# Seven products in place of eight: gate and up of a SwiGLU feed-forward by blocks of two by two

## The chip, the cores and the metric

The kernel runs on one core of one Trainium2 chip. The metric is the time of one execution on the device in microseconds (us). The core has a matrix engine (PE), a vector engine (DVE), a scalar engine (ACT), a general engine (POOL) and queues for transfers (DMA), the one of which SyncE fills (SP's) carries the weights. Each engine works through its own instructions in order and waits on semaphores for the others. SBUF is the on-chip memory of 128 partitions; PSUM holds the results of matmuls.

## The reference, cut to what matters

Two layers of mixer and feed-forward on 512 tokens of width 1024, then a last RMSNorm. The change is in the feed-forward part (`D_FF` = 2816):

```python
def rmsnorm(x, g):
    y = x * lax.rsqrt(jnp.mean(x * x, axis=-1, keepdims=True) + NORM_EPS)
    return y * g

def swiglu(xn, w_gate, w_up, w_down):
    return (jax.nn.silu(xn @ w_gate) * (xn @ w_up)) @ w_down

def reference(x, positions, ...):
    h = x
    for layer in range(DEPTH):                       # 2
        h = h + mixer(rmsnorm(h, mixer_norm_g))      # attention, not touched
        h = h + swiglu(rmsnorm(h, ffn_norm_g[layer]), ffn_w_gate[layer], ffn_w_up[layer], ffn_w_down[layer])
    return rmsnorm(h, final_norm_g)
```

## The kernel before, in words

Everything is kept transposed: `h` holds the residual stream as 8 tiles of 128 features by 512 tokens. Products are made of three matmuls: each operand is split into a rounded high part (one copy on ACT) and a low part (one subtraction on DVE), and high·high, high·low and low·high are summed in PSUM (`mm3`). `xo` holds the two parts of `h` times the norm's gain; the norm's factor per token is not in it. It is computed while the first product runs (`rstd_cols`, `rstd_rows`) and lies in `rbc`, 128 equal rows of 512 tokens.

Gate and up are made in 22 blocks `f` of 128 columns each. A block has two slabs of weights, gate and up, of 128 x 1024 numbers (8 pieces of K by 128 columns). `slab` loads one from HBM into `wraw` (512 KB, SP's queue, 2 buffers), ACT copies it to the high half of `whl` (4 buffers) and DVE makes the low half. Then 24 matmuls of 512 columns run into a bank `ps_g` (3 buffers). For gate DVE multiplies the bank by `rbc` into `gs`, ACT applies silu in place; for up DVE multiplies by `rbc` into `us`, multiplies that by `gs`, and ACT and DVE split the product into `ht[f]`. The down projection then sums over the 22 `ht` for each of 8 blocks `n` of outputs, and `residual` adds the bank to `h`. In the last layer the last block is done in two halves of 256 tokens (`final`).

The order of every engine's instructions is not the order of this code. `Sched.run` plans all of them: it walks through time with a cost for each instruction, takes on each engine the ready one with the highest rank (the longest costed path behind it, where PE's instructions keep the order in which they are written), gives out buffers in order, and emits the result. So a cost in the plan that differs from the chip's changes no result, but the order in which an engine's instructions wait on each other. Buffers of a feed-forward part lie in a memory scope that opens only when those before it are done with (the number behind the buffers in `tag`).

Of the kernel before, what the change touches and what calls it, by code (L numbers as in the profile page):

```python
# [62 lines left out]
class Sched:  # L63
# [32 lines left out]
    def run(self, opened, emit):  # L96
# [45 lines left out]
        while n_done < len(ops):  # L142
            best = None
            for e in "TVAGS":
                te = None
# [39 lines left out]
            if o.dma:  # L185
                eng[e] = st + cost
                dma_free = max(dma_free, st + cost + 600) + o.dma / 360.0
                end = dma_free + 900
# [66 lines left out]
def trunk(ctx, tc, xT, pos, consts_in, gv, lamv, wv0, wqk0, wo0, wgu0, wd0, wv1, wqk1, wo1, wgu1, wd1, out):  # L255
# [588 lines left out]
    def ffn(L, wgu, wd, gi_next):  # L844
        rbc = None
        ht = [buf(f"ht{L}") for _ in range(NF)]
        for f in range(NF):
# [33 lines left out]
        for n in range(NC):  # L881
# [17 lines left out]
    def final(n, ws, down):  # L899

        rb = buf("rbc1")

        def part(t0, tn):
# [25 lines left out]
            for c in (0, 4, 2, 6):  # L929
                o = buf("fo")  # L930
                for z in range(2):
                    src = lambda c=c, z=z: h.t[:, c + z, cols]
# [72 lines left out]
    def open_scope(sc):  # L1005
        if sc - 1 in stacks and sc > 1:
            stacks.pop(sc - 1).close()
        es = ExitStack()
        sb = es.enter_context(tc.tile_pool(name=f"sb{sc}", bufs=1))
        pp = es.enter_context(tc.tile_pool(name=f"pp{sc}", bufs=1, space=PSUM)) if sc == 0 else None  # L1010
        for t, (s, n) in tags.items():
            if s == sc:
                for i in range(n):
                    if shapes[t][0] is None:
                        phys[t, i] = "none"
                    else:
# [81 lines left out]
```

## Time and profile before

| | |
|---|---|
| runs | 1228.51, 1230.77, 1231.13 us; median 1230.77 us |
| profiled execution | 1229.38 us, of which the span is 1227.6 us |
| busy share of the span | PE 98%, DVE 55%, ACT 49%, POOL 12% |
| gate and up of layer 0 | from 250.85 us; its second block and those after it in the loop take 10.88 us each |
| down of layer 0 | 492 to 612 us |
| gate and up, down of layer 1 | 855 to 1094 us, to 1216 us |
| granted clock of PE | 1.00 (2.4 GHz) from 4 to 1219 us |

How to read it: times in the trace are from the span's start. "Idle before, releaser" beside a group is how long its engine stood just before these instructions and whose work ended that. The duration of a matmul in a row is longer than its distance to the next one, since matmuls overlap; what a row of many matmuls gives is the length of the whole run and their count.

### The profile page before, as it was taken

Reading aid. Unit: us, or ns where it says so; the run is one execution under the profiler, and the core shown is the slowest. Engines: PE = TensorE matmul, PEld = TensorE weight load, DVE = VectorE, ACT = ScalarE, POOL = GpSimd, SP = SyncE. Lnnn points to the kernel's source line nnn. Section 1 sums busy time; section 2 is a strip of 40 time slices with the busy share of each in tenths; the row PEclk is TensorE's granted clock in tenths of the full one; section 3 lists DMA queues with packets and bytes.
Section 4 is the critical chain, followed back from the end, with each engine's and each line's share of the span. In section 5 each row is a group of like instructions: output and inputs, shape, how many; then the busy total and the mean of one; then the engine's idle time right before and its main releaser. Section 6 shows DMA issues by size and latency. Waiting matters only on the chain.

```text
span 1227.6 us, 15958 instructions
## 1 busy us (share of the span) xinstructions
PE 1204.9 (98%) x5994; PEld 1014.3 (83%) x5994; DVE 672.8 (55%) x1404; ACT 598.8 (49%) x1039; POOL 150.9 (12%) x138
## 2 busy tenths in 40 slices
PE   9999999999999999999999999999999999999997
PEld 7889788888888888888897787888888888888887
DVE  7876987544444444333246988975444444443332
ACT  7877987542332323222357888875323323232221
POOL 1222331210000000000122334423000000000000
PEclk9999999999999999999999999999999999999998
DMA  8775755523233333333578657545232233333322
GB/s 252 185 171 140 162 136 113 138 86 102 87 103 91 98 103 97 97 95 95 132 182 180 144 132 172 117 124 137 86 103 89 100 101 89 103 93 97 95 77 69
DMA packets 47260, 146.49 MB, mean 119 GB/s; under 512 B 5840, under 2 KB 9040, under 8 KB 47184
## 3 DMA queue, kind: packets, MB, share of 16 engines
q1 hardware_dynamic: 38832, 116.08, 31.1%
q0 software_dynamic: 8064, 29.36, 13.8%
q8 instruction: 47, 0.77, 0.3%
q14 instruction: 29, 0.24, 0.1%
q10 hardware_dynamic: 288, 0.04, 0.0%
HBM read 134.98 MB, written 2.10 MB: 112 GB/s over the span
## 4 chain that ended last, share of the span: by engine, by line
PE 85%; DVE 8%; DMA 3%; issue 2%; ACT 1%; POOL 1%; SPq 0%; POOLq 0%; ACTq 0%; DVEq 0%
PE ps_g L351 75%; PE ps_s L351 3%; PE ps_o L351 2%; PE ps_t L351 2%; PE ps_t L354 2%; DMA kk<-kk 1%; DVE lg L716 1%; DVE lg L332 1%; DVE a L329 1%; DMA wraw<-wqk 1%; DVE kk L329 1%; DVE sh L675 1%; DVE lg L324 1%; DVE pt L329 1%; DVE qs L329 1%
## 5 line engine op out<-in xcount | busy, mean ns | idle before, releaser
L351 PE MATMUL ps_g<-xo,whl 128*128 128x512 f32 x2832 | 669.6, 391 | 0.0
L351 PEld LDWEIGHTS ps_g<-xo,whl 128*128 128x128 f32 x2832 | 526.3, 188 | 105.3
L320 ACT ACTIVATE whl<-wraw 128x1024 fp32r<-128x1024 f32 (+1 forms) x248 | 255.3, 1044 | 494.3 <-PE ps_g L351 357.6
L351 PE MATMUL ps_g<-ht,whl 128*128 128x512 f32 (+1 forms) x1122 | 241.3, 377 | 0.0
L351 PEld LDWEIGHTS ps_g<-ht,whl 128*128 128x128 f32 x1122 | 202.0, 188 | 38.6
L329 DVE TENSOR_TENSOR whl<-wraw,whl 128x1024 fp32r<-128x1024 f32 (+1 forms) x136 | 162.0, 1191 | 97.6 <-ACT whl L320 97.6
L329 DVE TENSOR_TENSOR us<-ps_g,rbc 128x512 f32<-128x512 f32 x44 | 30.4, 692 | 142.3 <-PE ps_g L351 142.3
L351 PE MATMUL ps_g<-whl,xo 128*128 128x256 f32 x672 | 92.4, 286 | 0.0
L351 PEld LDWEIGHTS ps_g<-whl,xo 128*128 128x128 f32 x672 | 86.5, 191 | 1.4 <-DVE xo L332 0.2
L329 DVE TENSOR_TENSOR gs<-ps_g,rbc 128x512 f32<-128x512 f32 x44 | 30.4, 692 | 98.8 <-PE ps_g L351 93.0
L346 ACT ACTIVATE lg<-lg,col 128x128 f32<-128x128 f32 (+3 forms) x128 | 70.9, 555 | 10.0 <-DVE col L716 8.8
L351 PE MATMUL ps_g<-ot,whl 128*128 128x512 f32 x288 | 73.6, 396 | 0.0
L329 DVE TENSOR_TENSOR h<-ps_g,h 128x512 f32<-128x512 f32 (+1 forms) x29 | 19.1, 671 | 89.2 <-PE ps_g L351 89.2
L351 PE MATMUL ps_s<-kk,qs 128*128 128x128 f32 (+3 forms) x256 | 62.1, 324 | 3.5 <-DMA kk<-kk 2.5
L351 PEld LDWEIGHTS ps_g<-ot,whl 128*128 128x128 f32 x288 | 52.9, 188 | 10.1
L389 POOL DMA_DIRECT2D whl<-wv x14 | 12.3, 882 | 373.4 <-ACT whl L320 372.4
L716 DVE CUSTOM_DVE_ANT_0 lg<-ps_s,cc 128x128 f32<-128x128 f32 (+3 forms) x96 | 45.4, 482 | 14.5 <-PE ps_s L351 11.6
L351 PEld LDWEIGHTS ps_s<-kk,qs 128*128 128x128 f32 x256 | 42.8, 189 | 12.5 <-DVE col L716 3.4
L329 POOL TENSOR_TENSOR fo<-h,rbc 128x256 f32<-128x256 f32 x4 | 2.9, 734 | 363.5 <-ACT rbc L320 363.5
L354 PE MATMUL ps_t<-cc,lg 128*128 128x128 f32 x240 | 40.5, 277 | 7.1 <-DVE lg L332 4.5
L329 DVE TENSOR_TENSOR pt<-ps_t,pt 128x128 fp32r<-128x128 f32 (+1 forms) x96 | 45.4, 480 | 2.4 <-ACT pt L320 1.7
L329 POOL TENSOR_TENSOR sh<-sh,sk 128x512 f32<-128x512 f32 x28 | 38.7, 1383 | 60.3 <-DVE sh L675 50.9
(135 smaller groups left out, 1065.1 us busy)
## 6 DMA issues: line engine op xcount, KB each, us to landing
wraw<-wgu SPq DMA_DIRECT2D x88, 512.0 KB, 3.5
wraw<-wd SPq DMA_DIRECT2D x32, 512.0 KB, 3.5
wraw<-wqk SPq DMA_DIRECT2D x30, 512.0 KB, 6.8
whl<-wqk POOLq DMA_DIRECT2D x30, 512.0 KB, 7.3
kk<-kk SPq DMA_DIRECT2D x64, 128.0 KB, 4.7
wraw<-wo SPq DMA_DIRECT2D x16, 512.0 KB, 4.8
wraw<-wv SPq DMA_DIRECT2D x14, 512.0 KB, 6.6
whl<-wv POOLq DMA_DIRECT2D x14, 512.0 KB, 7.6
```

Source lines behind the costliest of these rows:

```text
L320: A.activation(out_(), in_(), AF.Copy, scale=sc)
L324: V.tensor_scalar(out_(), in_(), sc, None, OP.mult)
L329: lambda e: E[e].tensor_tensor(out_(), a(), b(), o), r, w)
L332: op([("V", vtt(n, 1))], lambda e: V.scalar_tensor_tensor(out_(), a(), s(), b(), o0, o1), r, w)
L346: A.activation(out_(), in_(), f, scale=scale, **kw)
L351: lambda e: T.matmul(out_(), l(), r_(), start=start, stop=stop), r, w)
L354: op([("T", 108)], lambda e: T.transpose(out_(), in_(), ident()), r + [(cc, None)], w)
L389: op([("G", 1100)], lambda e: G.dma_start(w.t[:, 1, :], src, accum_op=OP.add), [(w, (1, 0))], [(w, (1, 0))], dma=2 * 1024 * 512)
L675: op([("V", vtt(512))], lambda e: V.stream_shuffle(sh.t, p.t, swap), P, [(sh, None)])
L716: op([("V", vtt(w) + 10)], lambda e: V.tensor_tensor_reduce(lg.t[:, :w], p.t[:, :w], mask[0]()[:, 512 - w:], -0.125, 3.0e38, OP.add, OP.mi ...
```

## The change

In layers 0 and 1 alike, blocks `f` = 2 to 16 (15 of 22) compute gate and up together as the product of a matrix of two by two blocks with another: A11, A12 are the two K halves of gate's slab, A21, A22 those of up's, and X11, X12, X21, X22 are the normed input cut into two halves of K (4 tiles each) and two of tokens (256 each). In place of eight products of blocks there are seven (`p1` to `p7`), each of 12 matmuls of 256 columns, with sums of weight blocks and of input blocks as operands:

- the sums of input blocks are made once for a layer, after block 0 (`sums_of_x`): 16 scaled copies of 256 columns on ACT into `hr`, 8 additions of 512 columns ("VG": on DVE or POOL, as the planner places them; here 6 and 2), and 8 splits of 512 columns into `tf`
- the sums of weight blocks are made for each block: up's slab lands in `wu`, and a POOL DMA that accumulates adds its second half to its first (256 KB, line 931); POOL makes three further sums of 512 columns (`s23`, `s4`). What is split into high and low is `w1` (gate as loaded), `w2` (`wu`), `w3` (`s23`), all three of 1024 columns in `whl`, and `w4` (`s4`, 512 columns, in `wf`)
- the seven products lie in 256 columns of seven banks (`ps_g` three times, `ps_s` twice, `ps_t`, `ps_o`); one copy on ACT and eight additions of 256 columns on DVE make gate into `cg` and up into `cu`. Then come gate times `rbc`, silu and the product with up, as before
- of blocks 2 to 5 the product is split into `hd` at once; of blocks 6 to 16 it stays in `hr` and is split into `hh` from block 17 on, when the buffers of the scheme are done with

Up is no longer multiplied by `rbc`, in any block. Instead the result of the down projection is, per token, before it is added to `h`: one more DVE instruction of 512 columns for each `n` (of 256 for each half of the last). In plain blocks DVE has one instruction fewer. The planner gets a delay for the accumulating DMA (`late`) and scopes that overlap.

```diff
     def ffn(L, wgu, wd, gi_next):
...
+        def plain(f):
...
-                tt("V", lambda g=g: g.t, lambda p=p: p.t, lambda: rbc.t, OP.mult, 512, [(p, None), (rbc, None)],
-                   [(g, None)])
...
+                    tt("V", lambda: g.t, lambda p=p: p.t, lambda: rbc.t, OP.mult, 512, [(p, None), (rbc, None)], [(g, 0)])
+                    func(lambda: g.t, lambda: g.t, AF.Silu, 512, SET, [(g, 0)])
+            tt("V", lambda: u.t, lambda: p.t, lambda: g.t, OP.mult, 512, [(p, None), (g, 0)], [(u, 0)])
+            parts(f, lambda: u.t, [(u, 0)])
...
+        def product(p, w, o, x):
+            for c in range(4):
+                for n, (a, b) in enumerate(((0, 0), (0, 1), (1, 0))):
+                    ap, tok = x(b, c)
+                    mm(lambda: p.t[:, :256], lambda a=a, c=c: w.t[:, a, o + c * 128:o + c * 128 + 128], ap, 256,
+                       c + n == 0, c == 3 and n == 2, [(w, (a, 0)), tok], [(p, None)])
+
+        def winograd(f):
+            a1, a2, s23, s4 = buf("wraw"), buf(f"wu{L}"), buf(f"s23{L}"), buf(f"s4{L}")
...
+            dma(lambda: a2.t, lambda: A2, (), [(a2, 0), (a2, 1)], 2 ** 19)
+            op([("G", 1100)], lambda e: G.dma_start(a2.t[:, k1], A2[:, k2], accum_op=OP.add), [(a2, 0)], [(a2, 0)],
+               dma=2 ** 19, late=4500.0)
+            dma(lambda: a1.t, lambda: A1, (), [(a1, 0), (a1, 1)], 2 ** 19)
+            w1, w3, w2, w4 = buf("whl"), buf("whl"), buf("whl"), buf(f"wf{L}")
...
+            both(w1, a1, 1024, halves(a1))
+            tt("G", lambda: s23.t[:, k1], lambda: a2.t[:, k1], lambda: a1.t[:, k1], OP.subtract, 512,
+               [(a2, 0), (a1, 0)], [(s23, 0)])
+            tt("G", lambda: s23.t[:, k2], lambda: a2.t[:, k2], lambda: s23.t[:, k1], OP.subtract, 512,
+               [(a2, 1), (s23, 0)], [(s23, 1)])
+            both(w3, s23, 1024, halves(s23))
+            tt("G", lambda: s4.t, lambda: s23.t[:, k1], lambda: a1.t[:, k2], OP.subtract, 512, [(s23, 0), (a1, 1)],
+               [(s4, None)])
+            both(w2, a2, 1024, halves(a2))
+            both(w4, s4, 512, [(s4, None)])
+            p1, p6, p2, p7, p5, p4, p3 = [buf("ps_" + n) for n in "gsgtgos"]
...
+            product(p1, w1, 0, xb(0, 0))
+            copy("A", u0, q(p1), 256, P(p1), [(u, 0)], psum=True)
+            product(p6, w3, 0, xt(1))
+            add(g1, u0, p6, (g, 1), [(u, 0)], OP.add)
+            product(p2, w1, 512, xb(1, 0))
+            add(g0, u0, p2, (g, 0), [(u, 0)], OP.add)
+            product(p7, w3, 512, xt(2))
+            add(u0, g1, p7, (u, 0), [(g, 1)], OP.add)
+            product(p5, w2, 0, xt(0))
+            add(u1, u0, p5, (u, 1), [(u, 0)], OP.subtract)
+            add(g1, g1, p5, (g, 1), [], OP.subtract)
+            product(p4, w2, 512, xt(3))
+            add(u0, u0, p4, (u, 0), [], OP.add)
+            product(p3, w4, 0, xb(1, 1))
+            add(g1, g1, p3, (g, 1), [], OP.subtract)
+            tt("V", lambda: g.t, lambda: g.t, lambda: rbc.t, OP.mult, 512, [(rbc, None)], halves(g))
+            func(lambda: g.t, lambda: g.t, AF.Silu, 512, SET, [(g, 0), (g, 1)])
+            if f < ND:
+                tt("V", lambda: u.t, lambda: u.t, lambda: g.t, OP.mult, 512, halves(g), halves(u))
+                parts(f, lambda: u.t, halves(u))
+                return
...
+            if f < NP or f >= NP + NS:
+                plain(f)
+                if f == 0:
+                    sums_of_x()
+            else:
+                x = winograd(f)
...
             p = buf("ps_g")
             down(n, ws, p, 0, 512)
-            residual(p, n)
+            t = buf(f"cu{L}")
+            tt("V", lambda t=t: t.t, lambda p=p: p.t, lambda: rbc.t, OP.mult, 512, [(p, None), (rbc, None)], [(t, 0)])
+            tt("V", lambda n=n: h.t[:, n, :], lambda t=t: t.t, lambda n=n: h.t[:, n, :], OP.add, 512, [(t, 0)], [(h, n)])
```

On PE, in the middle of layer 0's gate and up, two groups of 24 matmuls (one block: gate, then up) stood before:

```order
L351 MATMUL ps_g_0_82<-xo_0_64,whl_2_74 128x512 x24
L351 MATMUL ps_g_1_83<-xo_0_64,whl_3_75 128x512 x24
```

In the changed kernel the third block, the first of the scheme, and the start of the fourth stand there as follows (seven groups of 12 for a block; `xo` are input blocks as they are, `tf` sums of them, `whl` and `wf` the split weights):

```order
L358 MATMUL ps_g_0_82<-xo_0_64,whl_2_74 128x256 x12
L358 MATMUL ps_s_0_85<-tf0_0_2505,whl_3_75 128x256 x12
L358 MATMUL ps_g_1_83<-xo_0_64,whl_2_74 128x256 x12
L358 MATMUL ps_t_0_87<-tf0_0_2505,whl_3_75 128x256 x12
L358 MATMUL ps_g_2_84<-tf0_0_2505,whl_0_72 128x256 x12
L358 MATMUL ps_o_0_89<-tf0_0_2505,whl_0_72 128x256 x12
L358 MATMUL ps_s_1_86<-xo_0_64,wf0_0_2506 128x256 x12
L358 MATMUL ps_g_0_82<-xo_0_64,whl_1_73 128x256 x12
L358 MATMUL ps_s_0_85<-tf0_0_2505,whl_2_74 128x256 x12
```

What moved: a block has 84 matmuls of 256 columns in place of 48 of 512, into seven banks in place of two; `p6`, second in the block, already needs `w3` (`whl_3` in the first block), and `p5` and `p4` need `w2`.

On DVE, a block in the middle of layer 0's gate and up had these rows before (up's eviction and its product with gate, low part of a slab, low part of `ht`, gate's eviction, low part of a slab):

```order
L329 TENSOR_TENSOR us0_0_2568<-ps_g_0_82,rbc0_0_2564 128x512
L329 TENSOR_TENSOR us0_0_2568<-us0_0_2568,gs0_0_2565 128x512
L329 TENSOR_TENSOR whl_1_73<-wraw_1_71,whl_1_73 128x1024
L329 TENSOR_TENSOR ht0_3_2545<-us0_0_2568,ht0_3_2545 128x512
L329 TENSOR_TENSOR gs0_1_2566<-ps_g_1_83,rbc0_0_2564 128x512
L329 TENSOR_TENSOR whl_2_74<-wraw_0_70,whl_2_74 128x1024
```

In the changed kernel the rows of a later block of the scheme, interleaved with the last ones of the block before (`cu0_0`, `cg0_0` and the other way round for `_1`), are:

```order
L336 TENSOR_TENSOR cu0_1_2500<-cg0_1_2498,ps_t_1_88 128x256
L336 TENSOR_TENSOR whl_0_72<-wu0_1_2509,whl_0_72 128x1024
L336 TENSOR_TENSOR cu0_1_2500<-cu0_1_2500,ps_g_2_84 128x256
L336 TENSOR_TENSOR cg0_1_2498<-cg0_1_2498,ps_g_2_84 128x256
L336 TENSOR_TENSOR cu0_1_2500<-cu0_1_2500,ps_o_0_89 128x256
L336 TENSOR_TENSOR hd0_4_2483<-cu0_0_2499,hd0_4_2483 128x512
L336 TENSOR_TENSOR whl_1_73<-wraw_1_71,whl_1_73 128x1024
L336 TENSOR_TENSOR cg0_1_2498<-cg0_1_2498,ps_s_1_86 128x256
L336 TENSOR_TENSOR wf0_1_2507<-s40_1_2514,wf0_1_2507 128x512
L336 TENSOR_TENSOR cg0_1_2498<-cg0_1_2498,rbc0_0_2496 128x512
L336 TENSOR_TENSOR cg0_0_2497<-cu0_0_2499,ps_s_0_85 128x256
L336 TENSOR_TENSOR cu0_1_2500<-cu0_1_2500,cg0_1_2498 128x512
```

What moved: two slabs' low parts became three and a half (`whl_3` comes from `s23`, `whl_0` from `wu`, `whl_1` from `wraw`, `wf0_1` from `s4`), the two evictions of 512 columns became seven additions of 256 that each wait for one product and follow in PE's order, and the multiplication by `rbc` reads SBUF.

At the start of layer 0's gate and up, the stretch of DVE from the evictions of block 1 to the first additions of the scheme is this in the changed kernel (before, the rows of blocks 1 and 2 stood there as shown above):

```order
L336 TENSOR_TENSOR hr0_7_2492<-hr0_7_2492,hr0_4_2489 128x512
L336 TENSOR_TENSOR tf0_0_2505<-hr0_5_2490,tf0_0_2505 128x512
L336 TENSOR_TENSOR hr0_6_2491<-hr0_6_2491,hr0_7_2492 128x512
L336 TENSOR_TENSOR tf0_0_2505<-hr0_7_2492,tf0_0_2505 128x512
L336 TENSOR_TENSOR cg0_1_2498<-ps_g_1_83,rbc0_0_2496 128x512
L336 TENSOR_TENSOR whl_3_75<-s230_0_2511,whl_3_75 128x1024
L336 TENSOR_TENSOR whl_0_72<-wu0_0_2508,whl_0_72 128x1024
L336 TENSOR_TENSOR tf0_0_2505<-hr0_6_2491,tf0_0_2505 128x512
L336 TENSOR_TENSOR wf0_0_2506<-s40_0_2513,wf0_0_2506 128x512
L336 TENSOR_TENSOR hd0_0_2479<-cu0_0_2499,hd0_0_2479 128x512
L336 TENSOR_TENSOR wf0_1_2507<-s40_1_2514,wf0_1_2507 128x512
L336 TENSOR_TENSOR cu0_1_2500<-ps_g_2_84,cg0_1_2498 128x512
```

and these are POOL's rows of that stretch, in which it had none before:

```order
L336 TENSOR_TENSOR hr0_4_2489<-hr0_4_2489,hr0_5_2490 128x512
L336 TENSOR_TENSOR hr0_2_2487<-hr0_2_2487,hr0_3_2488 128x512
L336 TENSOR_TENSOR s230_0_2511<-wu0_0_2508,wraw_0_70 128x512
L336 TENSOR_TENSOR s230_0_2511<-wu0_0_2508,s230_0_2511 128x512
L336 TENSOR_TENSOR s40_0_2513<-s230_0_2511,wraw_0_70 128x512
L336 TENSOR_TENSOR s230_1_2512<-wu0_1_2509,wraw_1_71 128x512
L336 TENSOR_TENSOR s230_1_2512<-wu0_1_2509,s230_1_2512 128x512
L336 TENSOR_TENSOR s40_1_2514<-s230_1_2512,wraw_1_71 128x512
L336 TENSOR_TENSOR s230_0_2511<-wu0_2_2510,wraw_0_70 128x512
L336 TENSOR_TENSOR s230_0_2511<-wu0_2_2510,s230_0_2511 128x512
L931 DMA wu0_0_2508<-wgu0 128x512
```

What moved: from the eviction of block 0's up to `whl_3` (the first `w3`) DVE has six instructions (four are shown) on the sums of the input and the eviction `cg0_1`; the eviction of block 1's up, `cu0_1` from `ps_g_2`, stands behind `w3`, `w2` and four splits. POOL's sums for the blocks 2, 3 and 4 fall into the same stretch.

## Rows read from the trace of the kernel before

**Rows 1.** The page: span, busy times, chain by engine.

```profile
span 1227.6 us, 15958 instructions
PE 1204.9 (98%) x5994; PEld 1014.3 (83%) x5994; DVE 672.8 (55%) x1404; ACT 598.8 (49%) x1039; POOL 150.9 (12%) x138
...
PE 85%; DVE 8%; DMA 3%; issue 2%; ACT 1%; POOL 1%; SPq 0%; POOLq 0%; ACTq 0%; DVEq 0%
```

**Rows 2.** Windows: us, busy (instructions) by engine, PE's clock, DMA share, GB/s.

```profile
300.00:490.00 190.00, 190.00 (x840) 157.34 (x839) 87.20 (x104) 58.47 (x71) 0.00 (x0) 1.00 0.33 97
4.00:1219.00 1215.00, 1200.19 (x5980) 1011.64 (x5978) 669.88 (x1392) 596.75 (x1036) 148.80 (x131) 1.00 0.45 119
```

**Rows 3.** Timeline of PE in up/gate and in the last down block.

```profile
299.65 10.59 PE L351 MATMUL ps_g<-xo,whl 128*128 128x512 f32 x46
...
1212.31 3.88 PE L351 MATMUL ps_g<-ht,whl 128*128 128x256 f32 x31
```

**Rows 4.** Timeline of DVE in gate and up (block 0) and at the kernel's end.

```profile
263.81 0.69 DVE L329 TENSOR_TENSOR us<-ps_g,rbc 128x512 f32<-128x512 f32 x1 [1.21 <-PE ps_g L351]
264.61 0.69 DVE L329 TENSOR_TENSOR us<-us,gs 128x512 f32<-128x512 f32 x1
265.22 1.22 DVE L329 TENSOR_TENSOR whl<-wraw,whl 128x1024 fp32r<-128x1024 f32 x1
266.35 0.69 DVE L329 TENSOR_TENSOR ht<-us,ht 128x512 fp32r<-128x512 f32 x1
...
1216.83 0.42 DVE L329 TENSOR_TENSOR h<-ps_g,h 128x256 f32<-128x256 f32 x1 [3.59 <-PE ps_g L351]
...
1220.80 1.08 DVE L329 TENSOR_TENSOR fo<-h,ps_o 128x256 f32<-128x256 f32 x3 [1.19 <-PE ps_o L351]
1221.80 0.47 DVE L332 SCALAR_TENSOR_TENSOR fo<-h,gvt,ps_o 128x256 f32<-128x256 f32 x1
```

**Rows 5.** Timeline: DVE and POOL at work together, three places of the mixer.

```profile
133.62 2.38 DVE L329 TENSOR_TENSOR kk<-a,kk 64x512 fp32r<-64x512 f32 x2
...
133.68 1.78 POOL L329 TENSOR_TENSOR sh<-sh,sk 128x512 f32<-128x512 f32 x1 [6.81 <-DVE sh L675]
...
247.62 0.75 DVE L332 SCALAR_TENSOR_TENSOR xo<-h,gvt,xo 128x512 fp32r<-128x512 f32 x1
...
247.73 1.79 POOL L329 TENSOR_TENSOR acc<-acc,sq 128x512 f32<-128x512 f32 x1 [3.65 <-ACT sq L346]
...
33.55 1.27 DVE L329 TENSOR_TENSOR a<-ps_s,ck 128x512 f32<-128x512 f32 x2
...
33.44 1.31 POOL L329 TENSOR_TENSOR sh<-sh,sk 128x512 f32<-128x512 f32 x1 [2.45 <-DVE sh L675]
```

**Rows 6.** Costliest groups, shapes apart: busy and mean ns of one | idle before.

```profile
L320 ACT ACTIVATE whl<-wraw 128x1024 fp32r<-128x1024 f32 x232 | 241.8, 1057 | 448.5 <-PE ps_g L351 311.9 <-issue 117.3 <-DMA wraw<-wqk 13.9
L346 ACT ACTIVATE gs<-gs 128x512 f32<-128x512 f32 x44 | 27.0, 615 | 4.3 <-DVE gs L329 4.3
L389 POOL DMA_DIRECT2D whl<-wqk x30 | 26.4, 880 | 106.3 <-ACT whl L320 72.9 <-PE ps_g L351 23.0 <-ACT pt L320 10.3
L320 ACT ACTIVATE rbc<-ps_s 128x256 f32<-128x256 f32 x2 | 0.8, 384 | 4.8 <-PE ps_s L351 4.8
```

**Rows 7.** Timeline of PE and ACT at the start of layer 0's gate and up.

```profile
250.85 5.60 PE L351 MATMUL ps_g<-xo,whl 128*128 128x512 f32 x24
...
261.00 5.27 PE L351 MATMUL ps_g<-xo,whl 128*128 128x512 f32 x22
...
261.28 0.60 ACT L320 ACTIVATE rbc<-ps_s 128x512 f32<-128x512 f32 x1 [2.06 <-PE ps_s L351]
```

**Rows 8.** Waits (total us, times, longest) of DVE, 250 to 495 us, and of PE.

```profile
DVE us L329 <- PE ps_g L351: 71.2, 22, 3.9
...
PE ps_t L354 <- DVE lg L332: 4.5, 5, 1.3
```

**Rows 9.** DMA issues: number, KB each, us to landing.

```profile
wraw<-wgu SPq DMA_DIRECT2D x88, 512.0 KB, 3.5
...
whl<-wqk POOLq DMA_DIRECT2D x30, 512.0 KB, 7.3
```

More of the change, by code (lines that the diff above doesn't have):

```diff
@@ L187, in run @@
                 dma_free = max(dma_free, st + cost + 600) + o.dma / 360.0
[L188 removed]
+                end = dma_free + 900 + o.late
             else:
@@ L845, in ffn, with parts @@
         rbc = None
-        ht = [buf(f"ht{L}") for _ in range(NF)]
-        for f in range(NF):
-            gs = []
+        ht = {}
+        gain = lambda c: (lambda: gvt.t[:, (2 + L) * 8 + c:(2 + L) * 8 + c + 1])
+        lo_, up_ = slice(0, 256), slice(256, 512)
+        def parts(f, src, r):
+            t = ht[f] = buf(f"hd{L}" if f < ND else f"hh{L}")
+            split(lambda: t.t[:, 0, :], lambda: t.t[:, 1, :], src, 512, r, (t, 0), (t, 1), "V")
+        def plain(f):
+            nonlocal rbc
+            g, u = buf(f"cg{L}"), buf(f"cu{L}")
             for z in range(2):
@@ L869, in ffn @@
+        later = []
+        for f in range(NF):
+            if f == NP + NS:
+                for x in later:
+                    x()
+            if f < NP or f >= NP + NS:
[4 more added lines that the diff above has]
+                x = winograd(f)
+                if x is not None:
+                    later.append(x)
         table_set("natural_log_exp_and_others")
@@ L886, in ffn @@
             if gi_next is None and n == NC - 1:
-                final(n, ws, down)
+                final(n, ws, down, rbc)
                 break
@@ L897, in ffn, with final @@
                      scale=lambda n=n: gvt.t[:, 32 + n:33 + n], extra=1)
-    def final(n, ws, down):
-        rb = buf("rbc1")
+    def final(n, ws, down, rbc):
+        rb = buf("hr1")
         def part(t0, tn):
@@ L1003, in trunk, with open_scope @@
     stacks = {}
[L1005 to L1016, printed above, removed]
[L1017 to L1019 removed]
+    def open_scope(last):
+        for sc in range(max(stacks, default=-1) + 1 if stacks else 0, last + 1):
+            for k in CLOSES.get(sc, ()):
+                stacks.pop(k).close()
+            es = ExitStack()
+            sb = es.enter_context(tc.tile_pool(name=f"sb{sc}", bufs=1))
+            pp = es.enter_context(tc.tile_pool(name=f"pp{sc}", bufs=1, space=PSUM)) if sc == 0 else None
+            for t, (s, n) in tags.items():
+                if s == sc:
+                    for i in range(n):
+                        if shapes[t][0] is None:
+                            phys[t, i] = "none"
+                        else:
+                            phys[t, i] = (pp if t.startswith("ps_") else sb).tile(shapes[t][0], shapes[t][1],
+                                                                                  name=f"{t}_{i}")
+            stacks[sc] = es
     ctx.enter_context(tc.manual_schedule())
```

95 lines of the change are left out of this document (70 added, 25 removed).

## The prediction

> **What bounds the kernel now.** I read the page first: PE is busy 98% of the span and holds 85% of the chain that ended last [rows 1]. A share over the whole span hides stages, so next come the windows of gate and up, the stage that is changed. There PE is busy 190.00 of 190.00 us at a granted clock of 1.00 (2.4 GHz), while DVE is busy 46%, ACT 31%, POOL not at all, and transfers take 0.33 of their engines' time [rows 2]. Third, what one matmul costs: 46 of 512 columns take 10.59 us end to end; the last one's row would read 0.39, so one follows the other after (10.59 − 0.39)/45 = 0.2267 us. For 31 of 256 columns it is (3.88 − 0.28)/30 = 0.1200 us, with weights that alternate in the same way, high, high, low [rows 3]. Fourth, the waits: DVE waits for PE in nearly every block, 71.2 us in 22 times before up's eviction alone [rows 8]. So gate and up run at PE's pace, and each other engine has room. The question is how much of it the change uses.
>
> **PE: what is removed.** A block took 48 × 0.2267 = 10.88 us and takes 84 × 0.1200 = 10.08 us: only 0.80 us less, though an eighth of the columns is gone, since two matmuls of 256 take 0.240 us and one of 512 takes 0.227. 15 blocks in 2 layers: **−24.0 us**. Plain blocks, mixers and down keep their matmuls.
> The Trainium skill ("TensorE: Matmul & The Clock Gate", section "Wait — 56ns, not 53.3ns?") gives N/2.4 GHz plus about 2.5 ns from one warm matmul to the next: 215.7 ns for 512 columns and, an estimate, 109.2 ns for 256. By that a block would win 48 × 0.2157 − 84 × 0.1092 = 1.18 us, in all 35.4 us. The trace does not agree (226.7 and 120.0 ns in this kernel), and its rows make the sum.
>
> **DVE: does its loop fit into 10.08 us?** Each of its durations is taken from start to start. Additions of 256 columns follow each other after (1221.80 − 1220.80)/3 = 0.33 us, operations of 512 after 0.61 (264.61 to 265.22), low parts of 1024 after 1.13 (265.22 to 266.35) [rows 4]. A block of the scheme has 7 × 0.33 + 3 × 0.61 + 3 × 1.13 = 7.5 us. Silu (0.615 us [rows 6]) stands between two of its rows with one addition of 0.33 to cover it, and `w3`'s low part waits for ACT's high part; I take 0.8 us for both: 8.3 to 8.4.
>
> New is POOL at work beside it, three sums of 512 columns a block. Gate and up have no such pair now, the mixers do [rows 5]. At 133.6 two DVE operations of 512 elements, both inputs in SBUF, take 2.38 us with one POOL operation that starts among them; alone they would take 0.61 + 0.69 = 1.30. So POOL put in 1.08 us; it itself took 1.78 instead of 1.31, and at 247.7 1.79: it waited too. At 33.5 two DVE operations that read PSUM end after 1.27 us, and POOL's beside them after 1.31: no one waited. So a POOL sum costs DVE between 0 (if it falls on additions from PSUM or on DVE's idle time) and 1.08 us. Going through DVE's order of a block, with what DVE does at each place from PSUM or waits anyway, I find about 0.5 us covered on average: 3 × 0.57 = 1.7. The loop is then **10.1 us** (9.3 if POOL is nearly covered, 11.6 if never), practically PE's 10.08. This is the number on which the forecast hangs: at 10.56 nothing is left of the gain (15 × 10.56 + 4.8 of what follows = 15 × 10.88).
>
> The Trainium skill ("SBUF — State Buffer", section "Who interferes with whom") describes an exclusive lock: a DVE instruction with two SBUF inputs and a GpSimd one that reads SBUF block each other for whole instructions, one with at most one SBUF input does not contend. The rows agree (1.08 us put in, none beside PSUM). Taken strictly, each sum shuts DVE out for its whole duration and the kernel ends on the slow side; as a mechanism of this kernel, by rows, that is part of rival C.
>
> Blocks 2 to 5 also split `hd` at once: 4 × 0.61 = 2.4 us a layer. Against that stands slack: in a block paced by PE, `w3` can be ready some 6.9 us in (when `p2` frees a `whl` buffer, 4.3 in, then 1.06 on ACT, 1.13 on DVE and hand-overs) and is wanted at 11.5; about 2 us of these 4.6 are left after the start below. So the steady part costs 15 × 0.02 + 2.4 − 2.0 = 0.7 us a layer, **+1.4**.
>
> **The start of each layer.** Here the sums of the input come on top. In the run before, PE starts gate at 250.85, ends block 0 at 261.00 + 11 × 0.2267 = 263.5 and block 1 10.88 later, at 274.4; `rbc` ends at 261.9 [rows 7]. Then `p1`, `p6`, `p2`, `p7` of 1.44 each, so `p5` could start at 280.1. DVE: block 0's up is evicted from 263.8 on [rows 4]; with splits before it I count from 265.0. Up to the first `w3` stand six operations on the input's sums, `cg0_1` and the low part: 7 × 0.61 + 1.13 = 5.4 us; POOL's sums for blocks 2 and 3, six, put in 6 × 1.08 less 0.6 beside `cg0_1` = 5.9. So `w3` is there at 276.3, and `p6`'s third matmul wants it at 276.1. Behind it stand `w2` (1.13), four splits and `cu0_1` (5 × 0.61 = 3.05) and three POOL sums (3.24), 7.4 us together: `cu0_1` frees `ps_g_2` for `p5` at 283.7 to 284.1. PE stands 3.6 to 4.0 us; with 4.0, **+8.0** for both layers. Bounds: 0, if POOL's sums fall where DVE waits for ACT's high parts; 8 a layer, if ACT's 15 or so rows in this stretch put in as much again.
>
> **What is hidden.** ACT has 3.5 copies of 1.06, silu of 0.62 and a copy of 256 columns of 0.38 in a block, 4.7 of 10.08 us [rows 6]. POOL: 3 × 1.31 + 0.88 = 4.8. SP's queue loads the same two slabs a block (3.5 us to landing); the accumulating transfer is new, 256 KB where the mixer's 512 KB ones land after 7.3 us [rows 9]. It lies on the way from `wu` to `s23` to `w3`, but `wu` has three buffers, so it is issued about two blocks, 20 us, ahead; without that cover 7 us would come before each block. DMA's share rises from 0.33 to some 0.5. The 11 deferred splits (11 × 0.61 on DVE) fall into five plain blocks of 10.88 us that have less to do than before. The extra multiplication in down is hidden under the next `n`'s 66 matmuls, except at the end: in layer 0 half of 0.61, in `final` one of 256 columns, 0.42 [rows 4]: **+0.75** with the hand-over.
>
> **Sum.** 1229.4 (profiled) − 24.0 + 8.0 + 1.4 + 0.75 = 1215.6; the median of the runs lies 1.4 above the profiled one: **1217 us**.
>
> **The rivals.**
> *All hidden (B).* The start costs nearly nothing and POOL's sums fall on PSUM additions: 1229.4 − 24.0 + 0.75 + 1.4 = 1208 (1205 to 1213). For it: DVE was idle over half of the stage [rows 2]. Against it: the six POOL sums just where DVE is densest.
> *DVE's loop becomes the bound (C), slower than before.* POOL puts in its full 1.08 most times: with a loop of 10.8 us a layer takes 15 × 10.8 + 4.8 = 166.8 instead of 163.2, 7.2 us more in all: 1238 (1232 to 1246 for 10.6 to 11.1). One way to it: each sum shuts DVE's SBUF operations out for its whole 1.31 us, less the 0.5 covered, 3 × 0.8 = 2.4 in place of 1.7: a loop of 10.7, 165.3 a layer, 1235; of C's chance I give it 0.08. C decides from 10.56 on. For it: the first two pairs of [rows 5], and that each sum starts between low parts of 1024; against it: seven of 13 rows of DVE read PSUM.
> *Given back (D).* A loop of 10.3 to 10.5, or a start of 8 us a layer, or a clock that falls: 1225 to 1234. PE's longest wait now is 1.3 us [rows 8], and the clock stays at 1.00 through it [rows 2]; what it does after 4 us of idleness no row here shows.
>
> **Chances.** Forecast, 1213 to 1225: 0.45; B 0.20; C 0.20; D 0.15. What a measurement tells from no change is about 0.2%, 2.5 us, so 1228.3 to 1233.2 is the same. Faster is the forecast, B and a third of D: 0.70; same a half of D: 0.08; slower C and the rest: 0.22. The range that leaves 2 in 10 out is 1206 to 1237, half of C's weight above it and a little of B's below.
>
> **What would show it.** Right: in gate and up of the changed kernel 84 matmuls in about 10.08 us, PE waiting once in each layer near `p6` or `p5` for DVE's low part or eviction, a few us in all, and then full to block 16; DVE near 90% busy there, and its operations beside POOL longer than 0.69. Wrong by C: PE waits in every block, for `whl` from DVE (`w3`) or for a bank, DVE without idle time. Wrong by B: DVE waits for PE in each block, none the other way. Wrong in PE's term: a spacing of 256-column matmuls other than 0.120 us in these blocks (the windows count them). Wrong in the clock: a granted clock under 1.00 behind the start. Wrong in what is hidden: PE waits behind `s23` for the accumulating transfer.

## The result, and the profile after

The changed kernel takes 1239.48 us (median of 7 runs, 1236.95 to 1243.39) against 1231.43 us (7 runs, 1228.51 to 1235.25): 1.0065 times as long, with a 95% interval from 1.0049 to 1.0081. Its profiled execution lasted 1237.35 us. The page of it, where [rows 1] stood before:

```profile
span 1235.6 us, 18900 instructions
PE 1184.7 (96%) x7074; PEld 1045.1 (85%) x7074; DVE 881.7 (71%) x1675; ACT 670.5 (54%) x1177; POOL 327.6 (27%) x262
...
PE 51%; DVE 21%; issue 20%; ACT 3%; DMA 3%; POOL 1%; POOLq 0%; DVEq 0%; ACTq 0%
```

The span is 8.0 us longer though PE is busy 20 us less. PE's share of the chain that ended last fell from 85% to 51%; of the 34 points 13 went to DVE and 18 to "issue", time in which an engine waited for nothing that the profile shows. The stages come out of PE's timeline, where gate and up (`xo` as input) and down (`hd`) begin in the two layers:

```profile
252.57 5.60 PE L358 MATMUL ps_g<-xo,whl 128*128 128x512 f32 x24
...
497.09 3.11 PE L358 MATMUL ps_g<-hd,whl 128*128 128x512 f32 x13
...
857.44 1.75 PE L358 MATMUL ps_g<-xo,whl 128*128 128x512 f32 x7
...
1102.36 1.98 PE L358 MATMUL ps_g<-hd,whl 128*128 128x512 f32 x8
```

Gate and up take 244.5 us in layer 0 and 244.9 in layer 1; they took 241.2 in each before (250.85 to 492.1, and in layer 1 853.07 to 1094.31, where the table ahead has 855). That is 3.3 and 3.7 us. Layer 0's gate and up also begin 1.7 us later (252.57 against 250.85). That difference stands in the first mixer, whose code is not changed. Of it 0.7 us is a longer wait for a transfer, here before and after; the other 1.0 us is there already ahead of these rows.

```profile
45.39 0.50 PE L351 MATMUL ps_s<-kk,qs 128*128 128x128 f32 x2 [0.94 <-DMA kk<-kk]
```

```profile
47.08 0.50 PE L358 MATMUL ps_s<-kk,qs 128*128 128x128 f32 x2 [1.63 <-DMA kk<-kk]
```

The wait differs from kernel to kernel (0.9 to 4.6 us in the traces below); that the change has no part in it is likely, but not shown. What the change costs for certain lies in gate and up. The window that answers to the first of [rows 2], from the middle of layer 0, and PE's waits between 253 and 498 us:

```profile
320.00:420.00 100.00, 91.42 (x753) 89.58 (x752) 97.05 (x117) 40.55 (x55) 56.82 (x39) 1.00 0.43 112
...
PE ps_s L358 <- DVE whl L336: 11.2, 9, 1.7
PE ps_g L358 <- DVE cu L336: 2.1, 1, 2.1
```

DVE, busy 46% there before, is busy 97%, and POOL 57% where it had nothing to do. PE is busy 91% and waits for low parts of `whl`. The clock is 1.00, so it is not the clock (in layer 1 it falls once, behind the start, and costs 1.5 us; last section). How fast the blocks go is seen in the rows of `p3` (`ps_s` from `wf`) of two blocks, ten blocks apart:

```profile
308.74 1.60 PE L358 MATMUL ps_s<-xo,wf 128*128 128x256 f32 x12
...
421.28 1.60 PE L358 MATMUL ps_s<-xo,wf 128*128 128x256 f32 x12
```

112.54 us for ten, 11.25 us a block on average, where the forecast had 10.1; the ten take between 10.3 and 11.9. The reason stands in the rows of DVE, POOL and PE over one block and the beginning of the next:

```profile
331.62 3.15 DVE L336 TENSOR_TENSOR cu<-cu,cg 128x512 f32<-128x512 f32 x1 [0.37 <-ACT cg L353]
334.69 0.41 DVE L336 TENSOR_TENSOR cg<-cu,ps_g 128x256 f32<-128x256 f32 x1
335.02 1.21 DVE L336 TENSOR_TENSOR whl<-s,whl 128x1024 fp32r<-128x1024 f32 x1
...
339.22 1.21 DVE L336 TENSOR_TENSOR whl<-wraw,whl 128x1024 fp32r<-128x1024 f32 x1
...
341.89 0.41 DVE L336 TENSOR_TENSOR cg<-cu,ps_s 128x256 f32<-128x256 f32 x1
342.66 1.62 DVE L336 TENSOR_TENSOR hr<-cu,cg 128x512 f32<-128x512 f32 x1 [0.37 <-ACT cg L353]
...
344.54 1.99 DVE L336 TENSOR_TENSOR whl<-s,whl 128x1024 fp32r<-128x1024 f32 x1
...
346.78 1.97 DVE L336 TENSOR_TENSOR whl<-wu,whl 128x1024 fp32r<-128x1024 f32 x1
...
331.34 1.63 POOL L336 TENSOR_TENSOR s<-wu,s 128x512 f32<-128x512 f32 x1
332.60 1.60 POOL L336 TENSOR_TENSOR s<-s,wraw 128x512 f32<-128x512 f32 x1
...
341.50 0.90 POOL L931 DMA_DIRECT2D wu<-wgu  x1 [7.30 <-DMA wu<-wgu]
342.12 1.61 POOL L336 TENSOR_TENSOR s<-wu,wraw 128x512 f32<-128x512 f32 x1
343.81 1.64 POOL L336 TENSOR_TENSOR s<-wu,s 128x512 f32<-128x512 f32 x1
345.40 2.27 POOL L336 TENSOR_TENSOR s<-s,wraw 128x512 f32<-128x512 f32 x1
347.63 2.28 POOL L336 TENSOR_TENSOR s<-wu,wraw 128x512 f32<-128x512 f32 x1
...
334.21 0.40 PE L358 MATMUL ps_s<-tf,whl 128*128 128x256 f32 x2
336.28 1.44 PE L358 MATMUL ps_s<-tf,whl 128*128 128x256 f32 x10 [1.67 <-DVE whl L336]
337.56 1.59 PE L358 MATMUL ps_g<-xo,whl 128*128 128x256 f32 x12
```

The product of up and gate, 0.69 us by itself [rows 4], takes 3.15 us at 331.62: two of POOL's sums, one after the other, go past it (331.34 to 334.20). `w3`'s low part (335.02 to 336.23) stands two rows behind it, and the third matmul of `p6` waits for that 1.67 us. The other rows of this block have the durations of [rows 4]: 0.41, 0.68, 1.21. In the next block POOL makes four sums, and there the engines take turns: the product takes 1.62 us, the two low parts 1.99 and 1.97 in place of 1.21, and two of the sums 2.27 and 2.28. DVE has no idle time but 0.37 us ahead of each product, so it does not catch up.

What gathers the sums into runs of two and four stands ahead of them in POOL's own order: the issue of an accumulating transfer (L931) waits for up's slab, 7.30 us at 341.50, and the sums behind it start 0.6 us after it. All ten runs between 308 and 410 us begin so. The sum at 331.34 has its inputs when the one before it ends, at 327.7, and still starts behind the issue at 330.72. No kernel with the issue at another place was run.

### The profile page after: what moved, and what is told of

Same layout as the page of the kernel before. It is cut to its first block, busy times and chain, and to the rows that moved or that the text cites. A ratio compares the mean times of both kernels' runs of the same rounds, so it can differ in the third digit from the quotient of the medians.

```text
span 1235.6 us, 18900 instructions
## 1 busy us (share of the span) xinstructions
PE 1184.7 (96%) x7074; PEld 1045.1 (85%) x7074; DVE 881.7 (71%) x1675; ACT 670.5 (54%) x1177; POOL 327.6 (27%) x262
## 4 chain that ended last, share of the span: by engine, by line
PE 51%; DVE 21%; issue 20%; ACT 3%; DMA 3%; POOL 1%; POOLq 0%; DVEq 0%; ACTq 0%
PE ps_g L358 36%; PE ps_s L358 7%; DVE whl L336 4%; DVE hr L336 4%; PE ps_o L358 4%; PE ps_t L358 3%; DVE cu L336 2%; DVE cg L336 2%; PE ps_t L361 2%; DMA kk<-kk 2%; DVE lg L723 1%; ACT cg L353 1%; DVE lg L339 1%; DVE kk L336 1%; DVE a L336 1%
## 5 line engine op out<-in xcount | busy, mean ns | idle before, releaser
L358 PE MATMUL ps_g<-xo,whl 128*128 128x512 f32 (+1 forms) x2112 | 439.4, 356 | 0.4 <-DVE v L339 0.4
L358 PEld LDWEIGHTS ps_g<-xo,whl 128*128 128x128 f32 x2112 | 346.4, 189 | 50.0 <-DVE v L339 0.7
L336 DVE TENSOR_TENSOR whl<-wraw,whl 128x1024 fp32r<-128x1024 f32 (+1 forms) x106 | 128.3, 1211 | 87.5 <-ACT whl L327 87.3
L358 PE MATMUL ps_g<-hh,whl 128*128 128x512 f32 (+1 forms) x816 | 177.7, 377 | 0.0
L358 PEld LDWEIGHTS ps_g<-hh,whl 128*128 128x128 f32 x816 | 146.9, 188 | 28.0
L358 PE MATMUL ps_s<-tf,whl 128*128 128x256 f32 x360 | 52.9, 286 | 21.3 <-DVE whl L336 21.0
L358 PE MATMUL ps_g<-hd,whl 128*128 128x512 f32 (+1 forms) x306 | 68.6, 377 | 0.0
L358 PEld LDWEIGHTS ps_s<-tf,whl 128*128 128x128 f32 x360 | 46.0, 189 | 25.6 <-DVE whl L336 25.6
L358 PEld LDWEIGHTS ps_g<-hd,whl 128*128 128x128 f32 x306 | 55.2, 188 | 10.6
L336 DVE TENSOR_TENSOR cu<-ps_g,rbc 128x512 f32<-128x512 f32 (+1 forms) x17 | 11.2, 660 | 72.4 <-PE ps_g L358 72.4
L358 PEld LDWEIGHTS ps_g<-ot,whl 128*128 128x128 f32 x288 | 52.9, 188 | 10.1
L336 POOL TENSOR_TENSOR s<-wu,wraw 128x512 f32<-128x512 f32 x30 | 51.9, 1731 | 27.1 <-DVE whl L336 22.3
L931 POOL DMA_DIRECT2D wu<-wgu x30 | 26.7, 890 | 113.8 <-DMA wu<-wgu 112.6
```

The source lines that it names most:

```text
L336: lambda e: E[e].tensor_tensor(out_(), a(), b(), o), r, w)
L358: lambda e: T.matmul(out_(), l(), r_(), start=start, stop=stop), r, w)
L931: op([("G", 1100)], lambda e: G.dma_start(a2.t[:, k1], A2[:, k2], accum_op=OP.add), [(a2, 0)], [(a2, 0)], dma=2 ** 19, late=4500.0)
```

## The experiments

Theory **L**: each of POOL's three sums a block keeps DVE from its operations with two inputs in SBUF for some 1.06 us, and DVE's loop becomes the bound. Without that the loop is 8.0 us, an estimate from the rows above: from 334.69 to 342.66, 7.97 us, there are all rows of a block but the product, and a split of `hd` that takes as long. Rival **N**: DVE simply has too many instructions. Rival **T**: `w3` is late by the accumulating transfer or POOL's own pace. Beside these stands the norm factor in the down projection. Times are medians; ratios are to the kernel before, run beside each kernel (medians 1230.4 to 1231.5 us), with a 95% interval, and are not exactly the quotients of the medians.

**The sums on DVE.**

```diff
-            tt("G", lambda: s23.t[:, k1], ...
+            tt("V", lambda: s23.t[:, k1], ...        # and so the two that follow
```

> The three sums of weight blocks of each block of the scheme are made on DVE in place of POOL; nothing else is changed. Theory L (a POOL sum keeps DVE from its own SBUF operations for about 1.06 us, never covered): DVE's loop falls from 11.2 to 7.5 + 0.45 + 3 x 0.61 = 9.8 us, just under PE's 9.97; PE's waits for the low part of w3 go, gate and up take some 229 to 233 us a layer in place of 244.7, the time is 1207 to 1217 us. Rival N (DVE has simply too many instructions): three more make it worse, over 1245. Rival T (w3 is late because of the accumulating transfer and POOL's own pace): the waits stay at a block's beginning, 1230 to 1240.

Measured: 1207.58 us, 0.9796 [0.9776, 0.9816]. DVE got three more instructions a block, and the kernel is 32 us faster than the changed one. A window of it, and two groups of DVE's rows in the changed kernel and then in this one:

```profile
320.00:420.00 100.00, 100.00 (x844) 100.00 (x844) 95.37 (x163) 47.06 (x62) 6.98 (x8) 1.00 0.42 115
```

```profile
L336 DVE TENSOR_TENSOR whl<-wu,whl 128x1024 fp32r<-128x1024 f32 x30 | 50.6, 1686 | 0.0
L336 DVE TENSOR_TENSOR hr<-cu,cg 128x512 f32<-128x512 f32 x22 | 46.7, 2124 | 7.4 <-ACT cg L353 7.4
```

```profile
L336 DVE TENSOR_TENSOR whl<-wu,whl 128x1024 fp32r<-128x1024 f32 x30 | 36.6, 1221 | 0.0
L336 DVE TENSOR_TENSOR hr<-cu,cg 128x512 f32<-128x512 f32 x22 | 15.1, 686 | 0.7 <-ACT cg L353 0.7
```

PE is busy all the time; the product's mean falls from 2124 to 686 ns, the low part's from 1686 to 1221. N falls: more instructions, less time. The accumulating transfer is as before and PE no longer waits, so its landing is not what is late. POOL's own pace went away with the sums in this kernel; against that half of T stands the changed kernel's trace, in which all of DVE's waits from 300 to 420 us end with ACT's silu and none with POOL:

```profile
DVE hr L336 <- ACT cg L353: 2.6, 7, 0.4
DVE cu L336 <- ACT cg L353: 1.1, 3, 0.4
```

**No sums at all.**

```diff
-            tt("G", lambda: s23.t[:, k1], ...        # all three
-            both(w3, s23, 1024, halves(s23))
+            both(w3, a2, 1024, halves(a2))
...
-            both(w4, s4, 512, [(s4, None)])
+            split(..., lambda: a1.t[:, k2], 512, [(a1, 1)], ...)
```

> Leaves the three sums of weight blocks out: w3 is split from the loaded and accumulated slab wu, w4 from half of gate's slab, so the products are not those of the scheme; every other instruction stays, the accumulating transfer too. Theory L: DVE's loop is 8.0 us, PE never waits in the blocks of the scheme behind the first one, gate and up take 228 to 231 us a layer, the time is 1207 to 1213. Rival N: the loop stays over 9.97 and PE waits, 1225 to 1240. Rival T: PE waits for w3 as now if the transfer is what is late, 1230 to 1240; near theory L's time if POOL's pace is.

Measured: 1207.45 us, 0.9792 [0.9772, 0.9812]. `w3` and `w4` are split here from what is loaded, so the kernel's products are not those of the scheme. The accumulating transfer is still there and costs nothing. To make the sums on DVE (1207.58) costs the same as not to make them: with 9.8 us, an estimate (8.0 + 3 × 0.61), its loop is under PE's.

**One sum on DVE, two on POOL.**

```diff
-            tt("G", lambda: s4.t, lambda: s23.t[:, k1], lambda: a1.t[:, k2], OP.subtract, ...
+            tt("V", lambda: s4.t, lambda: s23.t[:, k1], lambda: a1.t[:, k2], OP.subtract, ...
```

> One of the three sums of a block (s4) goes from POOL to DVE, two stay: a dose between the changed kernel and the run with all three on DVE. Theory L, by 1.07 us put in for each POOL sum: the loop is 8.0 + 0.6 + 2 x 1.07 = 10.7 us (11.2 with three on POOL, 9.8 with none), some 5 us less in each layer's loop than in the changed kernel, so 1227 to 1231. Rival (it is one place, the wait of the product of up and gate behind two POOL sums in a row, that costs): the loop falls under 9.97 as soon as no two follow each other, 1207 to 1213.

Measured: 1230.71 us, 1.0003 [0.9991, 1.0015]. **One sum twice**, four on POOL:

```diff
             tt("G", lambda: s4.t, lambda: s23.t[:, k1], lambda: a1.t[:, k2], OP.subtract, ...
+            tt("G", lambda: s4.t, lambda: s23.t[:, k1], lambda: a1.t[:, k2], OP.subtract, ...
```

> The last of POOL's three sums is made twice, same result: the suspected cost one third more. Theory L: the loop goes from 11.2 to 12.3 us, some 11 to 13 blocks a layer at DVE's pace, 24 to 28 us in all: 1263 to 1268. If POOL's sums were covered or only their place before the product of up and gate counted, under 1245.

Measured: 1268.37 us, 1.028 [1.0246, 1.0313]. With no, two, three and four sums of a block on POOL the kernel takes 1208, 1231, 1239 and 1268 us. Both runs came where L put them, at the upper edge. The steps are not equal, and DVE alone does not make them: the planner gives each of these kernels another order; in both the clock dipped in gate and up (0.98 between 320 and 420 us with two sums, 0.97 between 300 and 450 with four), where the changed kernel's did not; and with four sums 12.2 us of PE's waits end with ACT's high parts, where the changed kernel has no such wait.

**POOL copies in place of the sums**, one input in place of two:

```diff
-            tt("G", lambda: s4.t, lambda: s23.t[:, k1], lambda: a1.t[:, k2], OP.subtract, 512, ...
+            op([("G", gtt(512))], lambda e: G.tensor_copy(s4.t, a1.t[:, k2]), ...     # and so the other two
```

> POOL copies 512 columns in place of each sum (one input from SBUF in place of two, same outputs and waits), so the products are not those of the scheme. Theory L in the form that any POOL instruction that reads SBUF holds DVE up: copies put about as much into DVE's loop for their duration as sums do, 1225 to 1240. Theory L in the form that only instructions with two inputs do: DVE's loop falls to 8.0, 1207 to 1213. Rival T (POOL's pace): between, by the copies' duration.

Measured: 1207.84 us, 0.9793 [0.9768, 0.9818]. **POOL writes zeros**, no input:

```diff
-            tt("G", lambda: s4.t, lambda: s23.t[:, k1], lambda: a1.t[:, k2], OP.subtract, 512, ...
+            op([("G", gtt(512))], lambda e: G.memset(s4.t, 0.0), ...                  # and so the other two
```

> POOL fills 512 columns with zeros in place of each sum (no input read, same outputs and waits), so the products are not those of the scheme. If only POOL's reads of SBUF collide with DVE's second input: nothing is put in, DVE's rows beside POOL keep 0.69 and 1.21 us, 1205 to 1210. If its writes do too: DVE's rows grow by the fills' durations as beside the copies (about 0.5 us each).

Measured: 1206.99 us, 0.9821 [0.9784, 0.9858]. Neither kernel's products are those of the scheme. The time doesn't tell the two apart, since PE paces both (by time alone the copies would have spoken for an effect of two inputs only); DVE's rows do. With copies (0.96 us each) the product of up and gate still takes 1484 ns; with the fills beside it, 685:

```profile
L336 DVE TENSOR_TENSOR hr<-cu,cg 128x512 f32<-128x512 f32 x22 | 32.6, 1484 | 4.4 <-ACT cg L353 4.3
```

```profile
L940 POOL MEMSET s<- 128x512 f32 x90 | 52.7, 732 | 45.1 <-DVE whl L336 45.1
L336 DVE TENSOR_TENSOR hr<-cu,cg 128x512 f32<-128x512 f32 x22 | 15.1, 685 | 0.0
```

So in these kernels POOL's reading collides, with one input too, and its writing alone puts in nothing. Copies collide and yet cost no time: DVE is busy 92 us of 100 beside them (79 beside the fills), so its loop stays under PE's 9.97 us.

```profile
320.00:420.00 100.00, 100.00 (x844) 100.00 (x843) 92.04 (x135) 48.47 (x61) 26.02 (x34) 1.00 0.43 117
```

**The sums in halves.**

```diff
-            tt("G", lambda: s4.t, lambda: s23.t[:, k1], lambda: a1.t[:, k2], OP.subtract, 512, ...
+            for a, b in ((0, 256), (256, 512)):
+                tt("G", lambda c=c: s4.t[:, c], ..., OP.subtract, 256, ...            # and so the other two
```

> Each of POOL's three sums is made as two of 256 columns, same result. The question is the cover that the prediction counted on: additions of DVE from PSUM that run beside a POOL sum. Such a half alone takes 0.73 us in this kernel. If hardly anything covers it, six halves put in some 6 x 0.65: a loop of 11.9 in place of 11.2, 1250 to 1260. If each half finds an addition of 0.33 beside it: 8.0 + 6 x 0.35 = 10.1, 1212 to 1220.

Measured: 1239.00 us, 1.004 [1.0017, 1.0062] (10 runs, 1231.37 to 1245.07): as with whole sums, between both expectations. The trace is of the slowest of the ten, and shows in an extreme form how a short piece doesn't find cover. DVE, POOL and PE around 300 us, and PE's windows behind that (us, PE busy, clock, DMA share, GB/s):

```profile
299.58 9.16 DVE L336 TENSOR_TENSOR whl<-wu,whl 128x1024 fp32r<-128x1024 f32 x1
...
299.02 1.78 POOL L336 TENSOR_TENSOR s<-wu,wraw 128x256 f32<-128x256 f32 x2
...
306.14 1.50 POOL L336 TENSOR_TENSOR s<-s,wraw 128x256 f32<-128x256 f32 x2
...
303.85 1.58 PE L358 MATMUL ps_t<-tf,whl 128*128 128x256 f32 x12
309.55 2.90 PE L358 MATMUL ps_g<-tf,whl 128*128 128x256 f32 x12 [4.12 <-DVE cg L336]
```

```profile
308.00:311.00 3.00, 1.46 (x7) 0.64 0.37 105
311.00:314.00 3.00, 3.00 (x16) 0.50 0.63 221
314.00:317.00 3.00, 3.00 (x21) 0.72 0.62 116
317.00:320.00 3.00, 3.00 (x28) 1.00 0.51 167
```

A low part of 1.22 us takes 9.16: twelve POOL instructions stand back to back from 299.02 to 307.6, behind the issue of an accumulating transfer at 298.46, and DVE's isn't let in between any two. PE waits 4.1 us for what stands behind it.

**A placed sum.** The first sum of a block waits for the first addition of `p5` two blocks earlier:

```diff
-               [(a2, 0), (a1, 0)], [(s23, 0)])
+               [(a2, 0), (a1, 0)] + [(x, 1) for x in us[-2:-1]], [(s23, 0)])
...
+            us.append(u)
```

> POOL's first sum of a block waits for the first addition of p5 two blocks earlier (from block 8 on), so that it starts just ahead of two further additions from PSUM on DVE. If a placed cover works: 0.5 to 0.7 us less a block in the 9 blocks that have it, 1228 to 1235. If cover fails even when placed: 1238 to 1243. The loop stays over PE's 9.97 us in either case.

Measured: 1237.60 us, 1.0045 [1.0028, 1.0062]. It lies between the two expectations and decides nothing. In its trace the first sum does not start behind `p5`'s additions but some 4.5 us later (additions from 372.55, sum at 377.20): at 376.59 stands the issue of an accumulating transfer, for which POOL had waited 6.5 us. Whether a sum would be covered if it did start there stays untried.

**Only the norm factor moved.**

```diff
-NP, NS, ND = 2, 15, 6
+NP, NS, ND = 22, 0, 6          # all blocks plain; `sums_of_x` is left out, too
```

> All 22 blocks are plain: only the other half of the change is left, up's norm factor applied to the result of down. Theory: PE's pace as before, DVE one instruction fewer in a block and one more in each n of down, hidden: 1231.4 plus 0.5 to 1, within 2 us of before. Rival: the multiplication in down is on the path between the layers and costs more than 3 us.

Measured: 1231.45 us, 0.9996 [0.9977, 1.0015]: nothing beyond the interval, as expected. The effect is the scheme's.

**More blocks, with the sums on DVE.**

```diff
-NP, NS, ND = 2, 15, 6
+NP, NS, ND = 2, 17, 8          # and 2, 18, 9
-... ("wf", [128, 2, 512], F32R, 2), ("wu", [128, 1024], F32, 3), ("s23", [128, 1024], F32, 2), ("s4", R5, F32, 2)
+... ("wf", [128, 2, 512], F32R, 2), ("wu", [128, 1024], F32, 2), ("s23", [128, 1024], F32, 1), ("s4", R5, F32, 1)
```

(With 18 blocks `wf` has one buffer as well.)

> Sums on DVE and 17 blocks of the scheme in place of 15 (wu with 2 buffers, s23 and s4 with one, 8 blocks split at once). By PE's pace each block more saves 0.91 us: 2 x 2 x 0.91 = 3.6 us under the run with 15, 1204, if fewer buffers make no wait. Rival: DVE's loop of 9.8 us has no room for the two further splits at once (0.61 each) or for s23's single buffer, then 1206 to 1212.

> Sums on DVE and 18 blocks of the scheme (wu 2 buffers, s23, s4 and wf one, 9 blocks split at once): by PE's pace 5.4 us under the run with 15, 1202. Rival: with one buffer of w4 its low part waits for the last product of the block before and comes late for the next, PE waits in every block, over 1207.

Measured: 1203.84 us, 0.9783 [0.9759, 0.9807], and 1199.82 us, 0.9754 [0.973, 0.9778]. Layer 0's gate and up with 18:

```profile
245.00:480.00 235.00, 235.00 (x1768) 225.37 (x1767) 216.15 (x347) 123.77 (x177) 27.27 (x26) 1.00 0.45 123
```

PE is busy throughout; fewer buffers made no wait. That is the fastest version, 2.5% under the kernel before. It lies 2 us under its expectation; why is not shown.

## Why the prediction was wrong, step by step

- **What bounds the kernel** (PE in gate and up) was right for the kernel before. Matmuls of 256 columns even come a little closer here: twelve in 1.41 to 1.43 us (337.56 and the rows after it in PE's timeline), 84 in 9.97 us, which is the distance of the blocks wherever PE sets the pace (no sums, sums on DVE). The gain of PE's term is 15 × (10.88 − 9.97) = 13.7 us a layer, 27.3 in all, where the sum had 24.0. The Trainium skill's spacing ("TensorE: Matmul & The Clock Gate", section "Wait — 56ns, not 53.3ns?") was rightly not used: by an estimate from it, 109.2 ns for 256 columns, a block would be 9.17 us.
- **The start** was right: 4.0 us a layer forecast, and PE waited 1.2 us at `p6`'s third matmul and 2.1 at `p5`, the two places named, 3.3 together. Here the forecast had put in the whole 1.08 us for each sum, less 0.6 once, and so it came: DVE's operations of 512 follow each other after 1.70 us, 1.09 more than the 0.61 of [rows 4]. With the sums on DVE PE waits at neither place.
- **DVE's own instructions** were right: 7.5 us (with seven additions from PSUM, as the order shows; the list of the change says eight), and 0.45 for silu (the product starts at 342.66, 0.77 behind an addition of 0.33) where 0.8 was taken; without POOL's sums the loop is 8.0.
- **The step that failed** is the cover: "Going through DVE's order of a block, with what DVE does at each place from PSUM or waits anyway, I find about 0.5 us covered on average: 3 × 0.57 = 1.7." The loop was 11.25 us. Less the 8.0, and 0.2 for the three splits of `hd` that fall into those ten blocks, three sums put in 3.05 us where 1.7 stood, about 1.0 each: nearly the whole 1.08 read from [rows 5] (without any cover, 8.0 + 3 × 1.08 is 11.2, and the text named 11.6 for that case). DVE's rows from 308 to 410 us, each one's distance to the next less the 0.33, 0.61 or 1.13 of [rows 4], tell two cases apart. In four runs of four sums the engines took turns: 2.6 to 3.3 us put in, 0.76 a sum. There additions of 0.33 from PSUM did cover a part, and the forecast's 0.57 was not far off. In six runs of two sums the product of up and gate stood behind both: 2.5 to 2.9 us put in, 1.38 a sum, more than the 1.08 that the forecast took for the most. So the error was to take each sum by itself, at an average place in DVE's order; they come in runs, behind the issue of a transfer, and a whole run can go past one operation.
- Over those ten blocks that is 112.5 in place of 99.7 us, a loss of 12.8 where the forecast had 0.7 for a layer. With 3.3 at the start, 16.1 us stand against the 13.7 gained: 2.4 of the 3.3 us by which layer 0's gate and up are longer. Most of the rest lies ahead of the first block of the scheme (0.3) and in it beyond the two waits (0.5).
- **Rival C** described what happened, with its place, DVE without idle time and PE waiting for `w3`, and its time (1238, range 1232 to 1246). It had 0.20. The Trainium skill ("SBUF — State Buffer", section "Who interferes with whom") would have weighed more: taken strictly it gave a loop of 10.7 and 1235; measured were 11.25 and 1239.5. The same section says that a POOL instruction that only writes does not contend, and the fills agree (685 ns beside them).
- **What is hidden** was hidden: PE waits nowhere for the accumulating transfer or the deferred splits, and the norm factor in down shows in no time (1231.45 with it alone); of the 0.75 us forecast for the end nothing is seen, as layer 1's gate and up end 8.05 us later than before and the span 8.0. What the forecast did not see is that waiting to issue that transfer gathers POOL's sums.
- The **clock** stayed at 1.00 in gate and up of layer 0. In layer 1 a sign that the forecast had named came: behind the two waits at the start the granted clock fell to 0.50 for a few us, and PE took 4.43 us from the start of `p5` to that of `p3` (891.40 to 895.83) in place of 2.91 in layer 0. Those 1.5 us are in layer 1's 3.7.

## What to carry to other kernels

Work moved to an idle engine is not free if a trace shows that it holds up the engine that is nearly full: add its whole price to that engine's loop first, and take off cover only where the order shows an instruction that surely runs beside it. Look also at what stands ahead of it in its own engine's order, since a wait there gathers it into runs. Here three cheap subtractions cost DVE some 3.1 us a block on POOL and, by an estimate (3 × 0.61), 1.8 on DVE itself, and that was the difference between 0.65% slower and 2% faster. When a loop comes out within a few per cent of the bound, as 10.1 against 10.08 did, the forecast is the loop's uncertainty, and the chance of the other side should be near one half.

## What the runs showed of the hardware that was not expected

- A DVE instruction with two SBUF inputs can be kept out by a whole run of POOL instructions that follow each other at once: 9.16 us for one of 1.22, with twelve halves of sums gone past it. In the changed kernel's start, by contrast, the two engines took turns (DVE operations of 512 every 1.70 us from 269.08 on, one POOL sum in each), and so they did in every run of four sums later, so both happen; what decides which is open.
- POOL's copy of 512 columns (one input, 0.96 us) holds DVE up too (the product's mean is 1484 ns beside it); beside its fill (0.73 us) the product takes 685 ns, as alone.
- In the kernel with halves PE's granted clock fell to 0.50 (1.2 GHz) for a few us after a wait of 4.1 us: twelve matmuls took 2.90 us in place of 1.58, and the clock was back at 1.00 from 317 us on. Such a long wait is not needed. In the changed kernel PE waits 1.2 and then 2.1 us at the start of either layer's scheme, with the same work around it. In layer 0 the clock stayed at 1.00 behind that and the next twelve matmuls took 1.65 us; in layer 1 it fell to 0.50 and they took 2.67. What decides is not shown.

```profile
279.46 1.44 PE L358 MATMUL ps_s<-tf,whl 128*128 128x256 f32 x10 [1.19 <-DVE whl L336]
...
285.89 1.65 PE L358 MATMUL ps_g<-tf,whl 128*128 128x256 f32 x12 [2.15 <-DVE cu L336]
```

```profile
884.96 1.44 PE L358 MATMUL ps_s<-tf,whl 128*128 128x256 f32 x10 [1.20 <-DVE whl L336]
...
891.40 2.67 PE L358 MATMUL ps_g<-tf,whl 128*128 128x256 f32 x12 [2.15 <-DVE cu L336]
```

```profile
892.00:894.00 2.00, 2.00 (x11) 0.50 0.64 114
```
